# Pair 7 of the second up stage as seven half-size products, in both MLPs

## The chip, the cores and the metric

The kernel runs on one core of a Trainium2 chip. The metric is the time of the device for one execution, in microseconds (us), median of several runs. The engines named below are TensorE (PE, with its weight loads PEld), VectorE (DVE), ScalarE (ACT), GpSimd (POOL) and SyncE (SP), which issues most loads.

## The reference, cut to what matters

The program is a decoder of two layers on 512 tokens of width 1024: a gated short convolution with an MLP, then an attention block with an MLP, all in float32. What the change touches is the MLP of both layers:

```python
def squared_relu_mlp(h, w1, w2):
    return jnp.square(jax.nn.relu(h @ w1)) @ w2

x = x + squared_relu_mlp(rms_norm(x, norm_mlp[layer]), mlp_w1[layer], mlp_w2[layer])
```

`h` is 512 x 1024, `w1` is 1024 x 4096 and `w2` is 4096 x 1024. After the first MLP the residual is normalised and projected with `w_kv` for the attention; after the second comes the last norm and the output.

## The kernel before, in words

Every matrix is split into a high and a low half-precision part, and a product is three matmuls: high x high, high x low, low x high. The weights come from HBM in float32 pieces; ACT writes the high part (L219, L239) and DVE the low part (L220, L240).

The hidden width of 4096 is done in two halves. Each half is an up stage of eight column pairs (256 columns of `w1` each) and a down stage of four parts, p = 0 to 3, each with eight chunks of the hidden width. The order is: up half 0, down half 0, up half 1, down half 1 (`first_half`, and then `mlp_down` again).

A column pair is made in one of two ways. The ordinary way (`pair`) is 8 chunks x 2 x 3 matmuls of 128 x 128 weights on 512 columns, into two banks of PSUM. The other (`seven`) treats weights and activations as 2 x 2 blocks and makes 7 products of half-size blocks in place of 8 (the scheme of Strassen and Winograd): 7 x 4 chunks x 3 matmuls on 256 columns, into three banks, A, C and E. For this it needs sums of blocks of the activations (made once, in the up stage of half 0), and sums of blocks of the weights (`block_sums`, three instructions on DVE per piece, L156 and L158), so that a weight piece is converted as 7 blocks x 2 chunks x 128 = 1792 columns in place of 1024. ACT copies some products out of PSUM (L694), and DVE adds them up (L709, L712, L716). The down stage works by seven products throughout.

Behind a pair, `put_relu` makes the squared ReLU: max or min on DVE (L661 after `seven`, L664 after `pair`), a square on ACT, three token sums on DVE, and the split into `rh` (ACT, L669) and `rl` (DVE, L670), which the down stage reads.

The tuple `UP_SEVEN` says which pairs of which half go by seven: before, none of half 0 and pairs 0, 2, 4 and 6 of half 1, in both layers. An ordinary pair in half 1 takes its two banks from set c, a seven takes A and C from set a and E from set b. The down stage takes banks a, a, b, b for p = 0 and 2, and c, c, d, e for p = 1 and 3.

Weight pieces stand in a list in order of use (`mlp_pieces`). Ordinary and block pieces have buffers of their own: three loaded and four converted ones of each kind. `ahead()` converts up to three block pieces or two ordinary ones ahead of their use, and `load_more` issues a load when a loaded piece has been converted. Each engine works its queue in order; the order is laid down before the run by a scheduler that may pull a later, ready instruction into a gap, unless `tc.issue_after` puts it behind a named one. That is how conversions of later pieces come early.

Around the down stage of half 1: in the first layer `done_a` adds squares for the next norm and splits the residual for `w_kv`; the last step of that norm's sum is `thirds` (L398), which a matmul of TensorE reads (L406). In the second layer `mid_b` turns finished parts token by token with transposes on TensorE (L1523) and copies on ACT (L1519, L1534), and the final norm's gains are loaded by POOL into a buffer (`rb`) that held sums of activations.

Of the kernel before, what the change touches and what calls it, by code (L numbers as in the profile page):

```python
# [11 lines left out]
F16 = mybir.dt.float16  # L12
# [11 lines left out]
SW = 256.0  # L24
# [27 lines left out]
def body(ctx, tc, x, rel_bias, norm_mix, norm_mlp, mlp_w1, mlp_w2, a_w_in, a_conv_w, a_w_out,  # L52
         kv_norm, w_kv, cmp_pe_k, cmp_pe_v, phi_k_w1, phi_k_w2, phi_v_w1, phi_v_w2,
         b_w_qg, b_w_o, final_norm, ident_c, onehot_c, out):
    nc = tc.nc
# [4 lines left out]
    work = ctx.enter_context(pool("work"))  # L60
# [5 lines left out]
    turn = [0]  # L66

    def bank(tag, shape=(128, 512)):
        n = {"a": 2, "b": 2, "c": 2, "d": 1, "e": 1}[tag]
        return psum.tile(list(shape), F32, name=tag, bufs=n)  # L70

    def acc():
        turn[0] += 1
        return bank("aabbcc"[turn[0] % 6])
# [14 lines left out]
    def mlp_pieces(layer):  # L89

        for half in range(2):
            for p in range(8):
                (blocks if p in UP_SEVEN[half] else block)(mlp_w1[layer], (8 * half + p) * 256, SW)
            for p in range(4):
                down_blocks(mlp_w2[layer], p, half)

# [8 lines left out]
            pieces.append(([v[c + k, :, :, c0:c0 + 256] for k in range(2)], None, scale))  # L105

    BY_SEVEN = ((2, 2), (3, 0), (3, 2))
    UP_SEVEN = ((), (0, 2, 4, 6))

    v = a_w_in[0].rearrange("(c p) (s n) -> c p s n", p=128, s=3)  # L110
    for c in range(8):
# [151 lines left out]
    def ahead():  # L263
        while pos["cv"] < len(pieces) and pos["cv"] < pos["use"] + (AHEAD2[0] if blocked(pos["cv"]) else AHEAD):
            yield from convert_piece()

    def drain(gen):
        for _ in gen:
            pass
# [3 lines left out]
    wk = [first.__enter__()]  # L273
# [164 lines left out]
    xs = new_split(wk[0], "x0")  # L438
# [72 lines left out]
    for p in range(4):  # L511
        pc, pu, pb = [], [], []
        if p == 0:
# [10 lines left out]
            cv = convert_piece()  # L524
# [44 lines left out]
        for i, dst in enumerate((pc, pu, pb)):  # L569
# [19 lines left out]
            for m in range(2):  # L589
# [9 lines left out]
                elif dst is pu:  # L599
                    if m == 0:  # L600
                        convs = []
                    v = ftile("cv_v", 2, S + 2)
# [8 lines left out]
                else:  # L611
                    b = ftile("cv_b", 2)
# [12 lines left out]
    xs = new_split(work, "xs")  # L625
    ss = SumSq()
# [15 lines left out]
    def small_w():  # L642
        return (wk[0].tile([128, 2, 256], F32, name="dn_w", bufs=1), wk[0].tile([128, 256], F32, name="dn_p", bufs=1))

    def mlp_up(xs, ss, rh, half, rb, sums, gname):
        turn[0] = 1

        def root_rows():
            nonlocal rb
            rb = row_tile(broadcast_rows(ss.r), math.sqrt(SR) / (SW * SX))  # L650

        def new_z():
            return wk[0].tile([128, 8, 256], F32, name="ml_z", bufs=2)

        def put_relu(p, ph, z):
            t = z[:, 0:4].rearrange("p (m k) n -> p m (k n)", m=2)
            if len(ph) == 1:
                r = rb.rearrange("p (k n) -> p k n", k=2)
                for op, o, v, w in ((OP.max, z[:, 2:4], z[:, 2:4], r), (OP.min, z[:, 0], z[:, 0], r[:, 0]),
                                    (OP.min, z[:, 1], ph[0], r[:, 1])):  # L660
                    DVE.scalar_tensor_tensor(o, v, 0.0, w, op0=op, op1=OP.mult)  # L661
            else:
                for m in range(2):
                    DVE.scalar_tensor_tensor(t[:, m], ph[m], 0.0, rb, op0=OP.max, op1=OP.mult)  # L664
            yield
            ACT.activation(t, t, AF.Square)
            token_sums(z)
            yield
            ACT.activation(rh[0][:, p], z[:, 1:8], AF.Copy)  # L669
            DVE.tensor_tensor(rh[1][:, p], z[:, 1:8], rh[0][:, p], op=OP.subtract)  # L670

        def seven(xs, z, post):

            ws = [next_piece(), next_piece()]
            cv = ahead()
            A, C, E = bank("a"), bank("a"), bank("b")

            def product(ps, i, first):
                a, b = i
                for c in range(4):  # L680
                    wh, wl = (u[:, c % 2, a - 1] for u in ws[c // 2])
                    if b >= 4:
# [12 lines left out]

            next(post, None)
            product(A, (1, 1), True)
            kept = keep(1, A)
            with tc.issue_after(kept.ins):
                next(cv, None)  # L700
            product(C, (4, 4), True)
            keep(5, C)
            product(A, (5, 5), False)
            kept = keep(2, A)
            with tc.issue_after(kept.ins):
                next(post, None)
                next(cv, None)
            product(E, (3, 3), True)
            DVE.tensor_tensor(z[:, 3], E[:, 0:256], kept_at[1], op=OP.add)  # L709
            product(A, (6, 6), False)  # L710
            kept = keep(3, A)
            DVE.tensor_tensor(z[:, 0], kept_at[3], kept_at[5], op=OP.add)  # L712
            with tc.issue_after(kept.ins):
                drain(post)
            product(C, (7, 2), False)
            DVE.tensor_tensor(z[:, 2], C[:, 0:256], kept_at[2], op=OP.add)  # L716
            drain(cv)
            product(A, (2, 7), False)
            return [A[:, 0:256]]

        def places():

            for pool_, name, n in 4 * ((wk[0], "up_s", 4),) + ((work, "ssacc", 1), (work, "sq", 1)) + 2 * ((work, "rb", 3),):
                yield pool_.tile([128, 4, 256], F16, name=name, bufs=n)

        held, post = None, iter(())
        if half == 0:
            ss.thirds()
        for p in range(8):
            if p in UP_SEVEN[half]:  # L730
                z = new_z()
                post = put_relu(p, seven(xs, z, post), z)
                continue
            drain(post)
            ph = [bank(" c c cbc"[p]) for _ in range(2)] if half else [acc(), acc()]
            mid = {1: {1: ss.rstd, 4: root_rows}}.get(p) if half == 0 else None
            pair(xs, ph, mid=mid)
            drain(ahead())
            if p == 0 and half == 0:
                held = ph  # L740
                continue
            if held:
                drain(put_relu(0, held, new_z()))
                held = None
            post = put_relu(p, ph, new_z())
            if p + 1 not in UP_SEVEN[half]:
                drain(post)
            if half == 0 and p >= 4:
                if p == 4:
                    at = list(places())  # L750
                    sums.extend([at[2 * k], at[2 * k + 1]] for k in range(4))
                form_sums(sums, p - 4, gname, new_z(), turned_sums)
        drain(post)
        turn[0] = 5
        return rb
# [90 lines left out]
            next(post)  # L846
        drain(post)

    def first_half(hp, xs, ss, gname):
        rh = tuple(hp.tile([128, 8, 7, 256], F16, name=n) for n in ("rh", "rl"))  # L850
        sums = []
        rb = mlp_up(xs, ss, rh, 0, None, sums, gname)
        mlp_down(rh, None)
        mlp_up(xs, ss, rh, 1, rb, sums, gname)
        return rh

    xkv, xq = None, None
    with pool("hidden_a") as hp:
        wk[0] = hp
        rh = first_half(hp, xs, ss, "mlp0")  # L860
        xkv = new_split(work, "xs")
        ss = SumSq()

        def done_a(p):
            for m in range(2):
                ss.add(X[:, 2 * p + m])
            for m in range(2):
                yield
                split_gain(xkv, 2 * p + m, X[:, 2 * p + m], "kv")

        mlp_down(rh, done_a)


    with pool("attn") as ap:
# [579 lines left out]
        for i in range(len(items) + 6):  # L1454
# [39 lines left out]
    xs = xm  # L1494
    ss = ss2


    with pool("hidden_b") as hp:
        wk[0] = hp
        rh = first_half(hp, xs, ss, "mlp1")  # L1500
        xsh, xsl = (work.tile([128, 2, D], F32, name=n) for n in ("xsh", "xsl"))
        xt = [(xsh, xsl)[t // 2][:, t % 2] for t in range(4)]
        fng = [work.tile([128, S], F32, name="rb", bufs=3) for _ in range(2)]
# [162 lines left out]
```

## Time and profile before

| | |
|---|---|
| median of three runs | 1084.83 us (1084.77 to 1084.89) |
| the profiled execution | 1085.08 us |
| its span, first to last instruction | 1083.3 us |
| TensorE busy | 1070.7 us, 99% |
| DVE busy | 947.1 us, 87% |
| ACT busy | 615.6 us, 57% |
| granted TensorE clock, mean | 0.998 |

The profile is of one execution. The span is what the trace covers; the rest of the 1085.08 us lies around it. A row of the chain of waits has a start, a duration and what ran. A row of a stretch has the busy time of each engine with the number of its instructions, then the granted clock, the busy share of the DMA engines and GB/s. A row of a timeline has a start, a duration, the engine, the line, the operation, output and inputs with their shape, a count, and in brackets the idle time of the engine before it with what ended it. Durations of neighbouring instructions on one engine overlap a little, so the time from start to start is what one costs.

### The profile page before, as it was taken

The numbers are of one execution on the slowest core, as the hardware profiler recorded it, in microseconds if no ns is written. First come the engines' busy times: TensorE is split into PE (matmuls) and PEld (weight loads), VectorE is DVE, ScalarE is ACT, GpSimd is POOL, SyncE is SP. The second block draws the span as 40 slices with busy tenths as digits, with TensorE's granted clock in tenths as the row PEclk, the third lists the DMA queues.
The fourth block names the chain that finished last, engine by engine and source line by source line (L and its number), as shares of the span: only waits on it lengthen the run. The fifth ranks groups of instructions, "written<-read, shape, count | busy, mean of one in ns | idle before, by whom it ended". The sixth has DMA issues, their size and how long they took to land.

```text
span 1083.3 us, 20976 instructions
## 1 busy us (share of the span) xinstructions
PE 1070.7 (99%) x8378; PEld 729.8 (67%) x8378; DVE 947.1 (87%) x1658; ACT 615.6 (57%) x962; POOL 67.9 (6%) x109
## 2 busy tenths in 40 slices
PE   9999999999999999999999999999999999999997
PEld 4446644446887768884867677775444788766886
DVE  5898756998999999989478899996999899999886
ACT  5663243665434575448577887874656533565353
POOL 1000000000000000000110104221000000000022
PEclk9999999999999999999999999999999999999999
DMA  8344125431334335203443442201553133422221
GB/s 259 114 147 130 40 86 167 143 112 35 120 117 136 98 100 175 98 22 97 126 138 102 141 138 81 60 21 59 161 159 108 58 109 119 125 92 85 97 80 79
DMA packets 117283, 117.45 MB, mean 108 GB/s; under 512 B 7117, under 2 KB 114337, under 8 KB 117185
## 3 DMA queue, kind: packets, MB, share of 16 engines
q1 hardware_dynamic: 114288, 110.77, 32.7%
q10 hardware_dynamic: 2512, 4.70, 1.4%
q8 instruction: 66, 1.08, 0.4%
q0 software_dynamic: 384, 0.63, 0.2%
q14 instruction: 33, 0.26, 0.1%
HBM read 110.22 MB, written 2.14 MB: 104 GB/s over the span
## 4 chain that ended last, share of the span: by engine, by line
PE 90%; DVE 4%; ACT 3%; issue 1%; POOL 1%; DMA 0%; ACTq 0%; DVEq 0%; POOLq 0%
PE c L801 7%; PE a L801 7%; PE c L410 6%; PE c L411 6%; PE c L412 6%; PE a L687 6%; PE b L801 5%; PE a L412 5%; PE a L410 5%; PE a L411 5%; PE b L412 4%; PE b L410 4%; PE b L411 4%; PE d L801 4%; PE c L1308 3%; PE e L801 2%
## 5 line engine op out<-in xcount | busy, mean ns | idle before, releaser
L219 ACT ACTIVATE whi<-wst 128x1792 f16<-128x1792 f32 x86 | 145.1, 1694 | 126.1 <-DVE wst L158 51.2
L801 PEld LDWEIGHTS <-whi 128*128 128x128 f16 x1768 | 173.0, 98 | 20.3
L220 DVE SCALAR_TENSOR_TENSOR wlo<-wst,whi 128x1792 f16<-128x1792 f32 x86 | 173.3, 2019 | 12.8 <-ACT whi L219 12.8
L240 DVE SCALAR_TENSOR_TENSOR wlo<-wst,whi 128x1024 f16<-128x1024 f32 (+4 forms) x124 | 136.4, 1107 | 24.3 <-ACT whi L239 24.0
L239 ACT ACTIVATE whi<-wst 128x1024 f16<-128x1024 f32 (+4 forms) x124 | 117.3, 954 | 70.6 <-PE a L411 22.2
L412 PEld LDWEIGHTS <-wlo 128*128 128x128 f16 x848 | 82.7, 98 | 92.2 <-DVE wlo L240 1.0
L410 PEld LDWEIGHTS <-whi 128*128 128x128 f16 x848 | 82.8, 98 | 84.9 <-ACT whi L239 0.7
L411 PEld LDWEIGHTS <-whi 128*128 128x128 f16 x848 | 82.9, 98 | 84.4
L801 PEld LDWEIGHTS <-wlo 128*128 128x128 f16 x884 | 86.5, 98 | 10.9 <-issue 0.4
L412 PE MATMUL c<-xsh,wlo 128*128 128x512 f16 x224 | 84.9, 379 | 0.0
L410 PE MATMUL c<-xsh,whi 128*128 128x512 f16 x224 | 84.9, 379 | 0.0
L411 PE MATMUL c<-xsl,whi 128*128 128x512 f16 x224 | 84.9, 379 | 0.0
L669 ACT ACTIVATE rh<-ml_z 128x1792 f16<-128x1792 f32 x32 | 54.2, 1693 | 53.0 <-DVE ml_z L164 53.0
L1295 ACT ACTIVATE at_p<-at_s,at_m 128x384 f32<-128x384 f32 (+3 forms) x128 | 71.1, 557 | 21.4 <-DVE at_m L1293 20.8
L158 DVE TENSOR_TENSOR wst<-wst 128x256 f32<-128x256 f32 x172 | 72.4, 427 | 2.8
L670 DVE TENSOR_TENSOR rl<-ml_z,rh 128x1792 f16<-128x1792 f32 x32 | 64.5, 2019 | 8.0 <-ACT rh L669 7.9
L801 PE MATMUL a<-rh,wlo 128*128 128x256 f16 x256 | 69.1, 273 | 0.0
L801 PE MATMUL a<-rh,whi 128*128 128x256 f16 x256 | 69.1, 273 | 0.0
L801 PE MATMUL c<-rh,whi 128*128 128x256 f16 x252 | 68.7, 273 | 0.0
L801 PE MATMUL c<-rh,wlo 128*128 128x256 f16 x252 | 68.7, 273 | 0.0
L801 PE MATMUL c<-rl,whi 128*128 128x256 f16 x252 | 68.7, 273 | 0.0
L156 DVE TENSOR_TENSOR wst<-wst 128x512 f32<-128x512 f32 x86 | 59.1, 690 | 10.7 <-DMA wst<-mlp_w_dram 10.3
(434 smaller groups left out, 2837.8 us busy)
## 6 DMA issues: line engine op xcount, KB each, us to landing
wst<-mlp_w_dram SPq DMA_DIRECT2D x160, 256.0 KB, 3.0
wst<-mlp_w_dram SPq DMA_DIRECT2D x48, 512.0 KB, 4.0
wst<-a_w_in_dram SPq DMA_DIRECT2D x12, 512.0 KB, 3.8
wst<-w_kv_dram SPq DMA_DIRECT2D x12, 512.0 KB, 3.8
wst<-a_w_out_dram SPq DMA_DIRECT2D x8, 512.0 KB, 3.4
wst<-b_w_qg_dram SPq DMA_DIRECT2D x8, 512.0 KB, 3.7
wst<-b_w_o_dram SPq DMA_DIRECT2D x8, 512.0 KB, 3.5
T<-ext_d ACTq DMA_DIRECT2D x6, 528.0 KB, 3.6
```

The source lines that it names most:

```text
L158: DVE.tensor_tensor(b[:, :, o], b[:, :, x], b[:, :, y], op=OP.add)
L219: ACT.activation(hi, b[:, :, 1:], AF.Copy, scale=sc)
L220: lows[0] = DVE.scalar_tensor_tensor(lo, b[:, :, 1:], sc, hi, op0=OP.mult, op1=OP.subtract)
L239: ACT.activation(hi[:, s:e], w, AF.Copy, scale=sc)
L240: DVE.scalar_tensor_tensor(lo[:, s:e], w, sc, hi[:, s:e], op0=OP.mult, op1=OP.subtract)
L410: PE.matmul(ps, w[0], xs[0], start=start, stop=False, **k)
L411: PE.matmul(ps, w[0], xs[1], start=False, stop=False, **k)
L412: return PE.matmul(ps, w[1], xs[0], start=False, stop=stop, **k)
L670: DVE.tensor_tensor(rh[1][:, p], z[:, 1:8], rh[0][:, p], op=OP.subtract)
L687: PE.matmul(ps[:, 0:256], l, r, start=first and c == 0 and n == 0, stop=c == 3 and n == 2, skip_group_check=not first)
L801: mm = PE.matmul(acc7[i], wl if n == 1 else wh, xl if n == 2 else xh, stop=c == closes[i] and n == 2, start=c == 0 and n == 0 and not othe ...
L1295: self.weighed = ACT.activation(self.p[:, w], lg[:, w], AF.Exp, bias=mn[:, j:j + 1], scale=-1.0, accum_out=l[:, br * 4 + h:br * 4 + h + 1])
```

## The change

`UP_SEVEN` gets an index for the layer, and pair 7 of half 1 joins the pairs that go by seven, in both layers; half 0 stays without. Pairs of half 1 now take turns between bank sets a and c, whichever way they are made: even pairs a, odd pairs c. So pair 7 by seven has A and C from set c, next to pair 6 with set a. The rest of the diff serves pairs by seven in half 0, which this kernel doesn't have: `early` is false and `behind` is pairs 4 to 7 as before. The buffers for sums are taken one pair at a time instead of all at once.

```diff
-                (blocks if p in UP_SEVEN[half] else block)(mlp_w1[layer], (8 * half + p) * 256, SW)
+                (blocks if p in UP_SEVEN[layer][half] else block)(mlp_w1[layer], (8 * half + p) * 256, SW)
-    UP_SEVEN = ((), (0, 2, 4, 6))
+    UP_SEVEN = (((), (0, 2, 4, 6, 7)), ((), (0, 2, 4, 6, 7)))
-        def seven(xs, z, post):
+        def seven(xs, z, post, tag):
-            A, C, E = bank("a"), bank("a"), bank("b")
+            A, C, E = bank(tag), bank(tag), bank("b")
...
-            drain(cv)
+            with nullcontext() if half else tc.issue_after(kept.ins):
+                drain(cv)
...
+        by_seven = UP_SEVEN[layer][half]
+        early = half == 0 and layer == 0 and by_seven
+        behind = range(1, 5) if by_seven else range(4, 8)
...
         for p in range(8):
-            if p in UP_SEVEN[half]:
+            own = half or by_seven and p >= by_seven[0]
+            tag = ("c" if tag == "a" else "a") if own else "bca"[p % 3]
+            if p in by_seven:
                 z = new_z()
-                post = put_relu(p, seven(xs, z, post), z)
+                post = put_relu(p, seven(xs, z, post, tag), z)
                 continue
             drain(post)
-            ph = [bank(" c c cbc"[p]) for _ in range(2)] if half else [acc(), acc()]
+            ph = [bank(tag) for _ in range(2)]
...
-            if p + 1 not in UP_SEVEN[half]:
+            if p + 1 not in by_seven:
                 drain(post)
-            if half == 0 and p >= 4:
-                if p == 4:
-                    at = list(places())
-                    sums.extend([at[2 * k], at[2 * k + 1]] for k in range(4))
-                form_sums(sums, p - 4, gname, new_z(), turned_sums)
+            if half == 0 and not early and p in behind:
+                sums.append(next(at))
+                form_sums(sums, p - behind[0], gname, new_z(), turned_sums)
```

## Rows read from the trace of the kernel before

**Rows 1.** The page: busy us, share of the span, instructions of each engine.
```profile
PE 1070.7 (99%) x8378; PEld 729.8 (67%) x8378; DVE 947.1 (87%) x1658; ACT 615.6 (57%) x962; POOL 67.9 (6%) x109
```

**Rows 2.** The chain of waits, behind the first MLP and in the second.
```profile
489.95 0.28 PE d L406 x12
...
977.89 3.93 PE a L687 x36
...
987.06 0.22 PE c L410
...
997.42 1.31 PE a L801 x12
...
1054.56 0.28 ACT xsl L1534
```

**Rows 3.** Stretches of the first MLP: pairs 6 and 7, four down parts.
```profile
389.29:408.82 19.53, 19.53 (x135) 12.91 (x133) 18.14 (x25) 13.77 (x16) 0.00 (x0) 1.00 0.30 99
408.82:427.16 18.34, 18.34 (x171) 16.44 (x169) 17.89 (x23) 10.75 (x9) 0.00 (x0) 1.00 0.51 158
427.16:445.50 18.34, 18.34 (x171) 16.43 (x169) 17.83 (x27) 7.47 (x7) 0.00 (x0) 1.00 0.39 130
445.50:463.84 18.34, 18.34 (x171) 16.45 (x169) 17.18 (x30) 9.21 (x9) 0.00 (x0) 1.00 0.34 115
463.84:482.18 18.34, 18.34 (x170) 16.39 (x168) 15.83 (x27) 6.31 (x8) 0.00 (x0) 1.00 0.01 2
```

**Rows 4.** Stretches of the second MLP: pair 6, pair 7, three down parts.
```profile
977.89:987.06 9.17, 9.17 (x85) 8.16 (x84) 9.13 (x15) 4.99 (x8) 0.00 (x0) 1.00 0.02 6
987.06:997.42 10.36, 10.36 (x50) 4.75 (x49) 10.12 (x12) 7.04 (x6) 2.27 (x3) 1.00 0.45 143
997.42:1015.76 18.34, 18.34 (x170) 16.44 (x169) 14.73 (x16) 8.05 (x7) 0.00 (x0) 1.00 0.20 63
1015.76:1034.10 18.34, 18.34 (x170) 16.52 (x169) 14.36 (x25) 7.51 (x16) 3.25 (x4) 1.00 0.26 88
1034.10:1054.80 20.70, 20.70 (x190) 18.53 (x189) 19.40 (x26) 11.07 (x20) 1.80 (x1) 1.00 0.31 103
```

**Rows 5.** The timeline of DVE, second MLP: what its steps cost.
```profile
979.78 1.28 DVE L664 SCALAR_TENSOR_TENSOR ml_z<-c,rb 128x512 f32<-128x512 f32 x2
...
986.58 0.41 DVE L716 TENSOR_TENSOR ml_z<-a,dn_w 128x256 f32<-128x256 f32 x1
986.92 1.01 DVE L661 SCALAR_TENSOR_TENSOR ml_z<-ml_z,rb 128x256 f32<-128x256 f32 x2
...
988.19 2.01 DVE L670 TENSOR_TENSOR rl<-ml_z,rh 128x1792 f16<-128x1792 f32 x1
...
1016.45 0.68 DVE L156 TENSOR_TENSOR wst<-wst 128x512 f32<-128x512 f32 x1
...
1017.97 0.42 DVE L767 SCALAR_TENSOR_TENSOR dn_w<-a,dn_p 128x256 f32<-128x256 f32 x1
```

**Rows 6.** The timeline of DVE, first MLP and the norm behind it.
```profile
408.56 1.22 DVE L240 SCALAR_TENSOR_TENSOR wlo<-wst,whi 128x1024 f16<-128x1024 f32 x1
...
423.74 1.28 DVE L240 SCALAR_TENSOR_TENSOR wlo<-wst,whi 128x512 f16<-128x512 f32 x2
...
473.90 2.02 DVE L220 SCALAR_TENSOR_TENSOR wlo<-wst,whi 128x1792 f16<-128x1792 f32 x1
475.84 0.42 DVE L780 TENSOR_TENSOR X<-X,dn_w 128x256 f32<-128x256 f32 x1
...
488.74 0.69 DVE L398 TENSOR_TENSOR rb<-sq 128x512 f32<-128x512 f32 x1
```

**Rows 7.** Whom DVE waited for, 977 to 1050: total us, times, longest.
```profile
DVE wst L156 <- DMA wst<-mlp_w_dram: 3.3, 2, 1.8
DVE wlo L220 <- ACT whi L219: 2.2, 1, 2.2
```

More of the change, by code (lines that the diff above doesn't have):

```diff
@@ L643, in small_w, with mlp_up @@
         return (wk[0].tile([128, 2, 256], F32, name="dn_w", bufs=1), wk[0].tile([128, 256], F32, name="dn_p", bufs=1))
-    def mlp_up(xs, ss, rh, half, rb, sums, gname):
-        turn[0] = 1
+    def mlp_up(xs, ss, rh, layer, half, rb, sums):
+        gname = f"mlp{layer}"
         def root_rows():
@@ L721, in places, with early_sums, move_sums @@
         def places():
-            for pool_, name, n in 4 * ((wk[0], "up_s", 4),) + ((work, "ssacc", 1), (work, "sq", 1)) + 2 * ((work, "rb", 3),):
-                yield pool_.tile([128, 4, 256], F16, name=name, bufs=n)
-        held, post = None, iter(())
+            tags = 4 * ((wk[0], "up_s", 4),) + ((work, "ssacc", 1), (work, "sq", 1)) + 2 * ((work, "rb", 3),)
+            for i in range(0, 8, 2):
+                yield [u.tile([128, 4, 256], F16, name=name, bufs=n) for u, name, n in tags[i:i + 2]]
+        def early_sums(c):
+            if c < 2:
+                sums.append(next(at))
+                form_sums(sums, c, gname, new_z(), turned_sums)
+            else:
+                staged_sums[c] = [u[:, 4 + c, 0:4] for u in rh]
+                form_sums(staged_sums, c, gname, new_z(), turned_sums)
+        def move_sums():
+            for c in (2, 3):
+                sums.append(next(at))
+                for u, v in zip(sums[c], staged_sums[c]):
+                    nc.gpsimd.dma_start(u, v)
+        at, staged_sums = places(), {}
+        by_seven = UP_SEVEN[layer][half]
+        early = half == 0 and layer == 0 and by_seven
+        behind = range(1, 5) if by_seven else range(4, 8)
+        held, post, tag = None, iter(()), ""
         if half == 0:
@@ L738, in mlp_up @@
             drain(ahead())
+            if early and p < 2:
+                for c in (2 * p, 2 * p + 1):
+                    early_sums(c)
             if p == 0 and half == 0:
@@ L745, in mlp_up @@
             post = put_relu(p, ph, new_z())
-            if p + 1 not in UP_SEVEN[half]:
+            if p + 1 not in by_seven:
                 drain(post)
-            if half == 0 and p >= 4:
-                if p == 4:
-                    at = list(places())
-                    sums.extend([at[2 * k], at[2 * k + 1]] for k in range(4))
-                form_sums(sums, p - 4, gname, new_z(), turned_sums)
+            if early and p == 2:
+                move_sums()
+            if half == 0 and not early and p in behind:
+                sums.append(next(at))
+                form_sums(sums, p - behind[0], gname, new_z(), turned_sums)
         drain(post)
@@ L847, in mlp_down, with first_half @@
         drain(post)
-    def first_half(hp, xs, ss, gname):
+    def first_half(hp, xs, ss, layer):
         rh = tuple(hp.tile([128, 8, 7, 256], F16, name=n) for n in ("rh", "rl"))
         sums = []
-        rb = mlp_up(xs, ss, rh, 0, None, sums, gname)
+        rb = mlp_up(xs, ss, rh, layer, 0, None, sums)
         mlp_down(rh, None)
-        mlp_up(xs, ss, rh, 1, rb, sums, gname)
+        mlp_up(xs, ss, rh, layer, 1, rb, sums)
         return rh
@@ L859, in body @@
         wk[0] = hp
-        rh = first_half(hp, xs, ss, "mlp0")
+        rh = first_half(hp, xs, ss, 0)
         xkv = new_split(work, "xs")
@@ L1499, in body @@
         wk[0] = hp
-        rh = first_half(hp, xs, ss, "mlp1")
+        rh = first_half(hp, xs, ss, 1)
         xsh, xsl = (work.tile([128, 2, D], F32, name=n) for n in ("xsh", "xsl"))
```

## The prediction

> **What bounds the kernel now.** I read the page first. TensorE is busy in 99% of the span and VectorE (DVE) in 87% [rows 1]. A busy TensorE says little by itself, so I went to the chain of waits around the second up stage of the second MLP. There every link is a matmul: the stretch of seven products of pair 6 starts at 977.89 us, pair 7 (full size) at 987.06, the down stage at 997.42 [rows 2]. So pair 6 costs 9.17 us and pair 7 10.36 us, and nothing stands between them. Third, the stretches: in all ten that I cut out of the two MLPs TensorE is busy for the whole stretch and the granted clock is 1.00 [rows 3, 4]. TensorE therefore sets the end, and a microsecond of its work that goes is a microsecond of the kernel, as long as the others keep up. The reader is to see in the same rows who is closest to not keeping up: DVE, with 9.13 of 9.17 us and 10.12 of 10.36 us in the up stage, and 17.89, 17.83 and 17.18 of 18.34 us in the first three quarters of the first MLP's down stage. ScalarE (ACT) has 7.04 of 10.36 us, and the DMA engines are at 0.51 of their time at the most.
>
> **The change, part by part.** (1) In both layers column pair 7 of the second up stage goes from 8 chunks x 2 x 3 = 48 matmuls of 512 columns to 7 products x 4 x 3 = 84 of 256 columns. The first took 10.36 us (216 ns each), the second takes what pair 6 takes, 9.17 us (109 ns each) [rows 2]: 1.19 us less per layer, 2.38 us for both. That is all that the change can give directly.
>
> One rule speaks against this. The Trainium skill, "TensorE: Matmul & The Clock Gate", section "Back-to-back issue gap", says that in a stream of weight loads and matmuls the sustained spacing is about 81 ns at 128 columns and 131 ns at 512. By that 48 long matmuls would take 6.3 us, and 84 at 256 columns, an estimate on the line between the two figures of the Trainium skill (98 ns), 8.2 us: the change would lose 1.9 us per layer. The rows show 216 and 109 ns, so the measurement decides and the rule falls here.
>
> (2) DVE gets more to do, for pair 7 of each layer. Its two weight pieces are now turned into seven block forms. Such a piece costs DVE three block sums, 1.52 us from the first sum at 1016.45 to the next instruction at 1017.97 [rows 5], and a low part of 1792 columns, 1.94 us from 473.90 to 475.84 [rows 6]: 3.46 us. An ordinary piece costs one low part of 1024 columns, 1.22 us as recorded at 408.56, or 1.14 without the overlap of 0.08 that the longer one shows (2.02 recorded). Two pieces: 6.92 - 2.28 = +4.64 us. The outputs: three adds that put the products together, 0.34 us each (986.58 to 986.92), and the three max/min steps of 1.27 us (986.92 to 988.19) in place of the two of 1.28 us at 979.78 [rows 5]: +1.01 us. Squares, token sums and the split into rh and rl stay. Together +5.65 us of DVE per layer, in which TensorE now spends 1.19 us less. DVE is thus asked for 6.84 us of its idle time per layer. This is the price of the edit, and the question is who pays it.
>
> (3) First MLP. Over pairs 6 and 7 and the down stage DVE is idle for 1.39 + 0.45 + 0.51 + 1.16 + 2.51 = 6.02 us [rows 3]. 6.84 are wanted: 0.8 us are missing. What is late next? The last down piece's low part starts at 473.90 and ends at 475.84; TensorE comes to it two chunks before the stage's end, at 482.18 - 2 x 2.29 = 477.6 [rows 3, 6]. So the lead is down to 1.8 us there already. Behind the down stage the norm's sum of squares follows, whose last step on DVE starts at 488.74 and takes 0.69 us, and TensorE's matmul on it starts at 489.95 [rows 2, 6]: 0.5 us of cover. In between DVE converts four later w_kv pieces (first at 408.56, last at 423.74, some 4.7 us) that TensorE needs only after 482 [rows 6]; they can move back, but not past the sum of squares altogether. The bounds of the stall in this layer: 0 if the idle time closes up and the w_kv work moves; 6.84 - 1.76 = 5.1 us if none of it does. I take the 0.8 us that the balance lacks, since the row of the whole stretch is the nearest.
>
> (4) Second MLP. Here DVE is idle for 0.04 + 0.24 + 3.61 + 3.98 + 1.30 = 9.17 us from pair 6 to 1054.80 [rows 4], 2.3 us more than is wanted. There are two soft spots. Two of the idle times, 3.3 us together, are waits for a weight load [rows 7]; a load starts only when DVE has finished with the buffer, so it may slip along with DVE and the wait come back. Without these 3.3 us the balance is 1.0 us short. And the chain passes from ACT's copy at 1054.56 straight to TensorE [rows 2]: there is no cover at that point, and whatever DVE and ACT still owe arrives at the end. DVE's one wait of 2.2 us for a high part [rows 7], however, is set by ACT's copies of transposes that TensorE makes, so there the chain starts afresh if DVE has caught up by then. Bounds: 0 and 6.8 us; I take 0.3 us, near the lower end, as the balance is positive.
>
> (5) Moved steps. The low and high parts of the first two down pieces now stand behind those of pair 7: the four buffers for converted block pieces hold pairs 6 and 7 when pair 6 runs, so at the start of the down stage two down pieces are converted and not four. The third is needed 2 x 4.59 = 9.2 us into the stage and DVE needs 3.46 us for each of two, so I cost this at nothing beyond (3) and (4); if DVE is 5.7 us late at that point, one piece is just in time. The loads of pair 7 become four DMAs of 256 KB for two of 512 KB: the same bytes, on DMA engines that are at 0.45 in that stretch [rows 4]. The final norm's gains (POOL's two loads) and ACT's scaled identity wait for the last reader of the sums' buffers, now the end of pair 7 instead of pair 6, 9.17 us later; they are first used when the down stage's first quarter is done, 18 us on, so nothing. ACT gets two longer conversions and four copies of a product. That is less than DVE's 5.65 us, since each of these has a dearer partner there, and ACT is idle for 3.32 us in pair 7's stretch and 10.29 us in the next [rows 4]: nothing. Pair 7 also adds an order on ACT: pair 6's squares stand behind the copy of pair 7's third product, and its rh behind that of the fifth, 3.9 and 6.6 us into the pair, with conversions of down pieces queued behind them. The down stage reads this rh at its seventh chunk, 13.8 us into it: nothing again.
>
> (6) The banks. Pair 7 takes its two accumulators from set c while pair 6's sit in set a, so its first product need not wait for pair 6's last DVE step. Their third bank is of set b for both; the down stage takes both b banks, and it reaches the one of pair 7 with its seventh product, 18 matmuls or 1.96 us into the stage. The product in it is complete 5.24 us into pair 7, so there are 9.17 + 1.96 - 5.24 = 5.9 us. DVE must have read it by then: cover enough unless DVE is late by nearly all of its extra work. Pairs 1, 3 and 5 stay in c. I cost it at nothing; gone, it would be 1 us or so.
>
> **The sum.** -2.38 + 0.8 + 0.3 = -1.3 us. The profiled execution took 1085.08 us (span 1083.3 and 1.8 around it), which gives 1083.8; the median of the three runs is 0.25 us lower, so 1083.5 us.
>
> **The rivals.** (A) *DVE hides everything*: both layers keep 1.19 us, 1082.4 us. For it: the 4.7 us of w_kv conversions that can move, and 9.17 us idle in the second MLP. Against: 6.02 < 6.84 in the first. (B) *A wait takes the place of the work*: DVE's idle time closes only by half, 3.0 us in the first layer and 4.6 in the second. The stalls are 3.8 - 1.8 = 2.0 us and 2.2 us, net +1.8: 1086.6 us; with a little more closed it comes out at 1085. For it: all listed idle times are waits for ACT or a load, so they are made by the order of the queues and not by lack of work. (C) *DVE becomes the bound*, the slower side: in the first MLP's down stage DVE's queue never catches up, as the lead of the last converted piece is down to 1.8 us before the change. The place is the last quarter of the down stage, the price 5.1 us there at most, and from 3.4 us of total stall less 2.38 the kernel is slower by 1 us, from 4.6 us by more than 0.2%. With 5.1 us in the first and 2.2 in the second: 1089.7 us. For it: 97% busy stretches. Against: the movable w_kv work. (D) *Half-size products run into their weight loads.* If a load of 97 ns no longer hid beside its matmul of 109 ns, 84 of both would take 17.3 us, 6.9 us more than the pair: up to 1098.7 us, and anything between. For it: the loads fill 8.16 of pair 6's 9.17 us. Against: TensorE is full all that time at 109 ns a product [rows 4], in a stretch of the very kind that is added, so this is all but excluded. By the estimate from the Trainium skill's section above it would be 1.9 us per layer and 1088.6 us.
>
> **How the numbers follow.** My forecast (partly eaten, gain 0.3 to 2.1 us) 0.42; A 0.27; B 0.17; C 0.13; D 0.01. A measurement of this kernel can tell about 0.2%, 2.17 us, from no change. Faster by that is A alone: 0.27. Slower by that is C, D and 0.02 of B, whose own figure lies just below it: 0.16. The rest, 0.57, is within. The range: low is A and 0.2 us for what else may shift, 1082.2; the high end takes in B up to just below its own figure, 1086.4, and leaves out most of C. The forecast's own range is 1082.7 to 1084.5.
>
> **What would show it.** Right: the chain shows pair 7 in 9.2 us with 84 products of set c and b; DVE above 98% busy from pair 6 to the end of the first down stage, short gaps of TensorE (together under 1 us) in its last quarter or at the sum of squares, and the w_kv conversions later than 425. A would show as no gap at all in either MLP. B and C show as gaps of TensorE released by a low part on DVE; if pair 7's first product waits, (6) is wrong. The prediction is wrong if TensorE's gaps in the two MLPs add up to over 3 us, or if the time changes by more than the gaps and 2.38 us explain, that is, in the attention between.

## The result, and the profile after

The changed kernel is slower: median 1092.26 us (1091.28 to 1094.15, six runs) against 1084.84 (1084.42 to 1085.17, six runs) for the kernel before on the same chip. The ratio is 1.0069, 95% interval 1.0058 to 1.0079. The forecast was 1083.5, with a range up to 1086.4. The profiled execution of the changed kernel took 1093.24 us, its span is 1091.5, 8.2 over the one before. Line numbers of the profile move by 28 in the lower part of the file: the down stage is now L829 (was L801), its sums L795 (L767), the transposes L1551 (L1523), the token copies L1547 and L1562 (L1519, L1534).

Where the 8.2 us arise, from the starts of the stages (before: [rows 2 to 4]; after: the stretches below):

| stretch | before | after | difference |
|---|---|---|---|
| start to pair 6, first MLP | 389.29 | 389.50 | +0.2 |
| pairs 6 and 7, first MLP | 19.53 | 21.40 | +1.9 |
| down stage, first MLP | 73.36 | 75.44 | +2.1 |
| norm and attention, to pair 6, second MLP | 495.71 | 496.16 | +0.45 |
| pairs 6 and 7, second MLP | 19.53 | 18.40 | -1.1 |
| the rest | 85.88 | 90.60 | +4.7 |

The page, engines (as [rows 1]): 1.9 us more on TensorE, though it has less to do, and 10 more on DVE.

```profile
PE 1072.6 (98%) x8450; PEld 737.4 (68%) x8450; DVE 957.3 (88%) x1678; ACT 620.6 (57%) x970; POOL 69.9 (6%) x109
```

Stretches after the change, in the columns of [rows 3] and [rows 4]: pairs 6 and 7 and four equal parts of the down stage of the first MLP; pairs 6 and 7 and three parts of the second, then the stretch in which its fourth down part begins.

```profile
389.50:410.90 21.40, 18.59 (x169) 16.36 (x168) 21.30 (x31) 13.71 (x17) 0.00 (x0) 1.00 0.51 161
410.90:429.76 18.86, 18.47 (x170) 16.29 (x169) 17.77 (x26) 9.39 (x7) 0.00 (x0) 1.00 0.21 69
429.76:448.62 18.86, 18.86 (x176) 16.88 (x174) 18.50 (x30) 9.64 (x10) 0.00 (x0) 1.00 0.43 138
448.62:467.48 18.86, 17.82 (x164) 15.72 (x162) 17.02 (x27) 8.28 (x9) 0.00 (x0) 1.00 0.27 88
467.48:486.34 18.86, 18.80 (x173) 16.57 (x172) 17.32 (x29) 8.23 (x10) 0.00 (x0) 1.00 0.09 29
...
982.50:1000.90 18.40, 18.40 (x170) 16.45 (x169) 16.42 (x23) 11.19 (x14) 0.00 (x0) 1.00 0.18 59
1000.90:1019.20 18.30, 18.30 (x170) 16.39 (x168) 17.82 (x26) 9.81 (x8) 3.22 (x3) 1.00 0.36 116
1019.20:1037.60 18.40, 18.39 (x168) 16.25 (x167) 17.84 (x26) 9.33 (x17) 2.85 (x3) 1.00 0.37 125
1037.60:1058.30 20.70, 20.70 (x188) 18.23 (x187) 19.47 (x31) 8.95 (x7) 1.68 (x2) 1.00 0.36 117
1058.30:1068.00 9.70, 6.89 (x49) 5.26 (x47) 9.63 (x13) 5.69 (x15) 4.96 (x4) 0.82 0.02 6
```

The reader is to see three things. In the first row DVE is busy for 21.30 of 21.40 us and TensorE is not. In the row at 982.50 pair 7 by seven gives what it should, 18.40 for 19.53, with no gap. In the last row the second MLP loses everything at one point, and the granted clock there is 0.82.

For whom TensorE waited (total us, times, longest): first the first MLP from 375 to 490, then the second. Before the change neither stretch had such a row.

```profile
PE a L687 <- ACT dn_p L694: 2.4, 1, 2.4
PE a L829 <- DVE wlo L220: 1.4, 2, 1.0
PE c L687 <- ACT dn_p L694: 0.4, 1, 0.4
...
PE c L829 <- ACT xsh L1562: 2.4, 1, 2.4
PE c L829 <- ACT xsl L1562: 0.5, 1, 0.5
```

From start to start of TensorE's matmuls the gaps are 5.1 us in the first MLP (2.5 in pair 6, 0.6 in pair 7, 2.0 in the down stage) and 3.1 in the second; there about 1.5 us more come from matmuls at the lower clock behind the gap. That is 9.7, less 2.4 for the fewer matmuls; 0.2 at the start and 0.45 in the norm and the attention make 8.0 of the 8.2.

The largest wait of the first MLP is a copy of ACT that stands in the queue behind something else. The timeline of ACT in pair 6:

```profile
385.10 1.14 ACT L239 ACTIVATE whi<-wst 128x512 f16<-128x512 f32 x2
390.29 1.70 ACT L669 ACTIVATE rh<-ml_z 128x1792 f16<-128x1792 f32 x1 [4.05 <-DVE ml_z L164]
393.14 1.15 ACT L239 ACTIVATE whi<-wst 128x512 f16<-128x512 f32 x2 [1.15 <-DMA wst<-w_kv_dram]
394.19 0.36 ACT L694 ACTIVATE dn_p<-a 128x256 f32<-128x256 f32 x1
```

TensorE's third product, which goes into the bank that is copied, waits for the copy at 394.19 (L694). Ahead of it stands a conversion of `w_kv` (393.14), which waits for its load, and ahead of that the `rh` of pair 5, which waited 4.05 us for DVE. DVE was late with that because it, too, had `w_kv` in its queue, here between the token sums of pair 5:

```profile
387.18 1.22 DVE L240 SCALAR_TENSOR_TENSOR wlo<-wst,whi 128x1024 f16<-128x1024 f32 x1
388.31 0.42 DVE L164 TENSOR_TENSOR ml_z<-ml_z 128x256 f32<-128x256 f32 x1
388.65 1.22 DVE L240 SCALAR_TENSOR_TENSOR wlo<-wst,whi 128x1024 f16<-128x1024 f32 x1
389.78 0.41 DVE L164 TENSOR_TENSOR ml_z<-ml_z 128x256 f32<-128x256 f32 x1
```

Before, these conversions were at 408.56 to 423.74 [rows 6]. Pair 7's pieces no longer pass through the ordinary buffers, so the `w_kv` pieces behind them in the list get the buffers a pair earlier, and the scheduler, which fills gaps with what is ready, puts them there.

The 1.4 us in the down stage are of the same kind, in DVE's queue. From 389 to 490 DVE waits 2.9 us for weight loads, 0.5 before the change, and both low parts for which TensorE waits stand behind block sums that had waited so. The longer one:

```profile
451.38 0.69 DVE L156 TENSOR_TENSOR wst<-wst 128x512 f32<-128x512 f32 x1 [1.80 <-DMA wst<-mlp_w_dram]
451.99 2.02 DVE L220 SCALAR_TENSOR_TENSOR wlo<-wst,whi 128x1792 f16<-128x1792 f32 x1
```

ACT had written the high part of this piece by 449.72. The load that the block sums wait for went out at 445.95, when DVE had given its buffer free: what is late on DVE comes back to it as a later load.

In the second MLP it is again ACT's queue, at the end of the third down part:

```profile
1056.18 3.28 ACT L219 ACTIVATE whi<-wst 128x1792 f16<-128x1792 f32 x2 [2.86 <-DVE wst L158]
1059.37 0.36 ACT L1547 ACTIVATE ml_z<-c 128x256 f32<-128x256 f32 x1
...
1061.59 0.43 ACT L1562 ACTIVATE xsl<-c 128x256 f32<-128x256 f32 x1
```

Two conversions wait for DVE's block sums; behind them stand the token copies that free the bank of the fourth down part. Their transposes were over at 1053.9, 5.5 us before. The same two conversions before the change, in ACT's timeline:

```profile
1049.00 3.28 ACT L219 ACTIVATE whi<-wst 128x1792 f16<-128x1792 f32 x2 [2.86 <-DVE wst L158]
```

They are 7.2 us later now, while TensorE is 4.3 us later there (its products go on behind the transposes at 1053.69, before at 1049.44): DVE is 2.9 us further behind, and all of it arrives at the first matmul into that bank.

### The profile page after: what moved, and what is told of

It is laid out like the page before. It is cut to its first block, busy times and chain, and to the rows that moved or that the text cites. A ratio compares the mean times of both kernels' runs of the same rounds, so it can differ in the third digit from the quotient of the medians.

```text
span 1091.5 us, 21172 instructions
## 1 busy us (share of the span) xinstructions
PE 1072.6 (98%) x8450; PEld 737.4 (68%) x8450; DVE 957.3 (88%) x1678; ACT 620.6 (57%) x970; POOL 69.9 (6%) x109
## 3 DMA queue, kind: packets, MB, share of 16 engines
q8 instruction: 66, 1.08, 0.4%
## 4 chain that ended last, share of the span: by engine, by line
PE 72%; DVE 19%; ACT 3%; issue 3%; DMA 2%; POOL 0%; SPq 0%; ACTq 0%; DVEq 0%; POOLq 0%
DVE wlo L220 6%; PE c L410 5%; PE c L411 5%; PE c L412 5%; PE a L410 5%; PE a L412 5%; PE a L411 4%; PE c L829 4%; PE a L829 4%; PE b L410 4%; PE b L411 4%; PE b L412 4%; PE b L829 3%; PE c L1336 3%; PE a L687 2%
## 5 line engine op out<-in xcount | busy, mean ns | idle before, releaser
L219 ACT ACTIVATE whi<-wst 128x1792 f16<-128x1792 f32 x90 | 151.7, 1692 | 147.6 <-DVE wst L158 64.8
L220 DVE SCALAR_TENSOR_TENSOR wlo<-wst,whi 128x1792 f16<-128x1792 f32 x90 | 181.4, 2021 | 11.6 <-ACT whi L219 11.5
L829 PEld LDWEIGHTS <-whi 128*128 128x128 f16 x1768 | 173.3, 98 | 20.9
L239 ACT ACTIVATE whi<-wst 128x1024 f16<-128x1024 f32 (+4 forms) x120 | 113.1, 951 | 70.4 <-PE a L411 22.2
L240 DVE SCALAR_TENSOR_TENSOR wlo<-wst,whi 128x1024 f16<-128x1024 f32 (+4 forms) x120 | 131.4, 1102 | 24.4 <-ACT whi L239 24.2
L410 PEld LDWEIGHTS <-whi 128*128 128x128 f16 x816 | 79.8, 98 | 81.1 <-issue 0.6
L411 PEld LDWEIGHTS <-whi 128*128 128x128 f16 x816 | 79.7, 98 | 81.1
L829 PEld LDWEIGHTS <-wlo 128*128 128x128 f16 x884 | 86.6, 98 | 16.4 <-DVE wlo L220 5.1
L158 DVE TENSOR_TENSOR wst<-wst 128x256 f32<-128x256 f32 x180 | 76.8, 434 | 2.3
L411 PE MATMUL c<-xsl,whi 128*128 128x512 f16 x192 | 72.8, 379 | 0.0
L412 PE MATMUL c<-xsh,wlo 128*128 128x512 f16 x192 | 72.8, 379 | 0.0
L410 PE MATMUL c<-xsh,whi 128*128 128x512 f16 x192 | 72.8, 379 | 0.0
L829 PE MATMUL c<-rh,whi 128*128 128x256 f16 x252 | 68.9, 274 | 2.8 <-ACT xsh L1562 2.4
L156 DVE TENSOR_TENSOR wst<-wst 128x512 f32<-128x512 f32 x90 | 62.4, 697 | 10.1 <-DMA wst<-mlp_w_dram 9.8
L829 PE MATMUL a<-rh,wlo 128*128 128x256 f16 x256 | 69.2, 273 | 1.4 <-DVE wlo L220 1.4
L829 PE MATMUL a<-rh,whi 128*128 128x256 f16 x256 | 69.1, 273 | 0.0
L829 PE MATMUL c<-rh,wlo 128*128 128x256 f16 x252 | 69.0, 274 | 0.1
L829 PE MATMUL c<-rl,whi 128*128 128x256 f16 x252 | 69.0, 274 | 0.0
```

What stands on the lines that cost most here:

```text
L156: DVE.tensor_tensor(b[:, :, 4:7:2], b[:, :, 0:1].to_broadcast(two), b[:, :, 2:0:-1], op=OP.add)
L158: DVE.tensor_tensor(b[:, :, o], b[:, :, x], b[:, :, y], op=OP.add)
L219: ACT.activation(hi, b[:, :, 1:], AF.Copy, scale=sc)
L220: lows[0] = DVE.scalar_tensor_tensor(lo, b[:, :, 1:], sc, hi, op0=OP.mult, op1=OP.subtract)
L239: ACT.activation(hi[:, s:e], w, AF.Copy, scale=sc)
L240: DVE.scalar_tensor_tensor(lo[:, s:e], w, sc, hi[:, s:e], op0=OP.mult, op1=OP.subtract)
```

## The experiments

Two causes stand against each other. Q: the order of the queues, that is, conversions that wait ahead of copies that TensorE needs. V: DVE's amount of work, wherever it is put. A third, that the rest of the diff costs something, falls with the traces of the first two runs: outside the layer that has the new pair every engine runs the same operations on the same tiles in the same order as in the kernel before (l1_only up to 970 us, l0_only behind its first MLP), and the first MLP of l1_only takes 92.9 us from pair 6 to the end of its down stage, as before. All times are medians of 5 to 11 executions beside the kernel before, which lay at 1084.98 to 1085.08.

**Each layer alone.**

```diff
-    UP_SEVEN = (((), (0, 2, 4, 6, 7)), ((), (0, 2, 4, 6, 7)))
+    UP_SEVEN = (((), (0, 2, 4, 6, 7)), ((), (0, 2, 4, 6)))     # l0_only
+    UP_SEVEN = (((), (0, 2, 4, 6)), ((), (0, 2, 4, 6, 7)))     # l1_only
```

> Pair 7 by seven in the first MLP alone; the second MLP as before. Theory Q (the order of ACT's queue: conversions that wait for a load or for DVE stand ahead of a copy that TensorE needs) and theory V (VectorE lacks 5.65 us per layer, wherever it is put) both give here what the changed kernel lost up to the attention, 4.8 us less 0.4 us of start: 1084.8 + 4.4 = 1089.2 us, with gaps of TensorE of about 5 us in pairs 6, 7 and the down stage and none in the second MLP. If the two layers act on each other, it lies over 1 us off this.

> Pair 7 by seven in the second MLP alone. Both theories: the second layer's share of the loss, 8.2 - 4.8 = 3.4 us, 1088.2 us, with one group of gaps of about 3 us behind the second down part and the lower granted clock after it, and none in the first MLP. With l0_only it should add up to the changed kernel: 4.4 + 3.4 = 7.8 us over before.

1088.47 us (ratio 1.0033, 1.0022 to 1.0044) and 1086.68 (1.0014, 1.0005 to 1.0023): +3.4 and +1.6, each under what was expected, and together 5.0 of the 7.4. In l1_only the gaps are 2.6 us, and the lower clock doesn't come behind them. The trace of l0_only shows the other reason. It has the gap of 2.6 us in pair 6, but no gap of the down stage; in its place TensorE runs at the lower clock behind the gap. The same stretch, first of the changed kernel, then of l0_only:

```profile
395.00:398.00 3.00, 3.00 (x30) 2.68 (x29) 3.00 (x5) 2.63 (x4) 0.00 (x0) 1.00 0.19 68
```
```profile
395.00:398.00 3.00, 3.00 (x16) 2.06 (x15) 3.00 (x5) 2.05 (x4) 0.00 (x0) 0.50 0.23 81
```

One execution gets through 30 matmuls in 3 us, the other through 16. The 1.7 us lost there look like time for DVE to catch up: in copies_first, too, the lower clock follows this gap and the first MLP has no later one. No run separates the two. So an execution pays part of its loss at one place or at another, and the loss by stages differs between executions.

**w_kv held back.** ACT's conversions of the first four `w_kv` pieces behind its copy of pair 7's fifth product:

```diff
             kept = keep(3, A)
+            kept7[0] = kept.ins
...
-                ACT.activation(hi[:, s:e], w, AF.Copy, scale=sc)
+                with tc.issue_after(kept7[0]) if kv_at <= i < kv_at + 4 else nullcontext():
+                    ACT.activation(hi[:, s:e], w, AF.Copy, scale=sc)
```

> The changed kernel, with ACT's conversions of the first four w_kv pieces tied behind its copy of pair 7's fifth product, so that they can't stand in pairs 5 and 6; nothing else is changed. Theory Q: the gaps of 2.5 and 0.6 us in pairs 6 and 7 go, and the shorter ones in the down stage (2.0 us together) stay or grow by up to 1 us, since the same DVE work now lies there: 1089.2 to 1090.2 us. Theory V: the same work on DVE, so the stall only moves into the down stage: 1092.3 us, within 0.6.

1090.14 us (1.0044, 1.0032 to 1.0057): 2.1 below the changed kernel, as Q said, at the upper end. Stretches from pair 6 to the norm, and TensorE's waits:

```profile
389.20:407.50 18.30, 18.30 (x169) 16.41 (x168) 17.63 (x25) 12.21 (x15) 0.00 (x0) 1.00 0.21 69
...
426.25:445.00 18.75, 18.75 (x174) 16.80 (x173) 18.75 (x30) 10.08 (x12) 0.00 (x0) 1.00 0.44 143
445.00:463.80 18.80, 18.69 (x172) 16.52 (x170) 18.80 (x30) 9.20 (x9) 0.00 (x0) 1.00 0.45 143
463.80:482.60 18.80, 17.98 (x164) 15.64 (x162) 18.70 (x32) 8.01 (x9) 0.00 (x0) 1.00 0.17 52
```
```profile
PE c L829 <- DVE wlo L220: 0.8, 1, 0.8
PE d L406 <- DVE rb L398: 0.5, 1, 0.5
```

Pairs 6 and 7 now take 18.30 us without a gap: the order was what cost 3.1 us there. But in the last three of these stretches DVE is busy for 56.25 of 56.35 us, and TensorE waits for it. From the start of pair 6 to the end of the norm behind the down stage the layer takes 108.8 us, for 112.0 in the changed kernel and 107.7 before: the order took 3.2 us. What is left, 1.1 us more than before and the 1.19 us of the gain, goes with waits for a DVE that is hardly idle.

**Token copies first.** In the second MLP, the conversions behind the token copies in the third down part too:

```diff
-                        behind = squared if p == 1 else None
+                        behind = squared if p < 3 else None
```

> The changed kernel, with ACT's conversions that follow in the second MLP's third down part tied behind the token copies of that part (as they are already in the second part); nothing else is changed. Theory Q: TensorE's gap of 3.1 us at the fourth down part goes and with it the 1.5 us at the lower clock, less up to 1 us for conversions that now come later: 1087.7 to 1088.7 us. Theory V: DVE is what is late, and the gap comes back some microseconds later at a low part: 1091.5 to 1092.5 us.

1089.67 us (1.0045, 1.0033 to 1.0058), between the two. The gap at the fourth down part is gone, and 10 us later a smaller one comes up, where the transposes wait for DVE's sums of part 2:

```profile
PE a L1551 <- DVE X L808: 1.7, 1, 1.7
PE a L1551 <- DVE X L810: 0.3, 1, 0.3
PE c L829 <- DVE dn_w L1585: 0.3, 1, 0.3
```

**Both, then with less work for DVE.** both_held has the two edits. held_pool adds GpSimd for pair 7's block sums; held_nolow leaves out pair 7's low parts; after_nolow does that in the changed kernel's own order.

```diff
-                block_sums(b)
+                block_sums(b, POOL if i in fifth else DVE)                  # held_pool
...
-            lows[0] = DVE.scalar_tensor_tensor(lo, b[:, :, 1:], sc, hi, op0=OP.mult, op1=OP.subtract)
-            ready[i] = (hi, lo)
+            if i not in fifth: lows[0] = DVE.scalar_tensor_tensor(lo, ...)  # held_nolow, after_nolow
+            ready[i] = (hi, lo or hi)
```

> The two edits of kv_held and copies_first together; all work is done. From their traces: with w_kv held the first layer still takes 1.1 us more than before from pair 6 to the attention (108.8 against 107.7), with the copies first the second takes 1.3 us more to the end (106.9 against 105.6). If the two don't act on each other: 1085.0 + 2.4 = 1087.4 us, 0.5 either way. If a purely ordering cause remained (theory Q as first stated), it would be 1082.5.

> As both_held, with the block sums of pair 7's two pieces of each layer on GpSimd in place of VectorE: DVE is relieved of 3.0 of the 5.65 us per layer, all work is done. If what is left after the ordering is DVE's amount of work (theory V): the stalls of about 2.3 and 2.5 us per layer shrink by what DVE is relieved of, 1082.6 to 1084.0 us, a gain over before. If GpSimd's sums come late (a sum of 128x256 on it takes 0.7 to 2.3 us) or slow DVE beside them: 1087 to 1090 us, with TensorE waiting for pair 7's weights.

> As both_held, but the low parts of pair 7's weights are not made in either layer: TensorE reads the high part in their place, the same number of matmuls. DVE is relieved of 2 x 1.94 = 3.9 of the 5.65 us per layer and of nothing else. Theory V: the stalls left go and both layers show the 1.19 us of the fewer matmuls: 1082.4 to 1083.2 us. If it is not DVE's amount of work, it stays at both_held, 1087.4 us.

> The changed kernel in its own order, with the low parts of pair 7's weights left out as in held_nolow. Theory V (only the amount counts): as held_nolow, 1082.4 to 1083.2 us. Theory Q: the w_kv conversions still wait for their load ahead of the product copy, and pair 6 keeps its gap of 2.5 us (with the lower clock after it 4.2), while the stalls in the down stages go: 1085.3 to 1087.0 us.

1089.86 us (1.0044, 1.003 to 1.0058), 1088.86 (1.004, 1.0027 to 1.0052), 1085.55 (1.0006, 0.9997 to 1.0014) and 1091.07 (1.0057, 1.0045 to 1.007).

both_held misses its 1087.4: it is no better than either edit alone. Its trace has the 1.7 and 0.3 us of copies_first, and then the lower clock. The stretch behind that wait, first in copies_first, then in both_held:

```profile
1068.00:1072.00 4.00, 4.00 (x38) 3.61 (x39) 1.00 (x3) 2.93 (x13) 2.65 (x4) 1.00 0.00 0
```
```profile
1068.00:1072.00 4.00, 4.00 (x23) 2.95 (x22) 0.91 (x1) 2.80 (x13) 2.77 (x4) 0.57 0.01 2
```

held_pool has the same waits of TensorE as both_held, within 0.1 us, and one of 0.3 us more. So its 1.0 us is not shown to come from GpSimd: the lower clock is in the trace of both_held and not in this one.

held_nolow takes 3.9 us per layer from DVE and gains 4.3 us in all over both_held: amount counts. Two things go with it that no run separates: pair 7's low parts need no buffers either, and the lower clock of both_held is missing. after_nolow takes away the same work and gains 1.2, and 5.5 us lie between it and held_nolow: order counts as much. In its trace one row holds nearly the whole loss of the first MLP; it is again the copy of a first product, now pair 7's, and ahead of it in ACT's queue stands pair 6's `rh`, which waited 5.13 us for DVE's token sums:

```profile
PE c L687 <- ACT dn_p L694: 3.9, 1, 3.9
```
```profile
400.65 0.69 DVE L156 TENSOR_TENSOR wst<-wst 128x512 f32<-128x512 f32 x1 [4.10 <-DMA wst<-mlp_w_dram]
401.26 0.42 DVE L164 TENSOR_TENSOR ml_z<-ml_z 128x256 f32<-128x256 f32 x1
...
401.77 1.70 ACT L669 ACTIVATE rh<-ml_z 128x1792 f16<-128x1792 f32 x1 [5.13 <-DVE ml_z L164]
```

I had expected that gap in pair 6; it moved to the next pair. And here DVE is not busy: it stands idle for 4.10 us at block sums that wait for their load, with the last token sum behind them. That load went out at 395.67, behind one of `w_kv` at 395.25 in SP's queue, which had waited for DVE to finish a `w_kv` piece; in held_nolow it went out at 393.11, and the block sums found it there. So the order counts in three queues, ACT's, DVE's and that of the loads.

Neither Q nor V alone gives these four times. Both count: DVE is late, by its work or by a wait in its own queue, and an order in which ACT's queue passes its lateness on to copies needed at once makes several microseconds of it. Even held_nolow, with 1.8 us per layer more on DVE than before, shows nothing of the 2.4 us. In its second MLP TensorE waits 0.8, 0.3 and 0.3 us at the places of copies_first; what that edit costs without the added work on DVE was not run.

**Another place.** The fifth seven in half 0 in place of half 1, as pair 5 (with `own = half` and `early = False`, so that half 0 keeps its bank sets), in one layer or both:

```diff
+    UP_SEVEN = (((), (0, 2, 4, 6)), ((5,), (0, 2, 4, 6)))      # half0_l1; half0_l0, half0_both alike
```

> Pair 7 of half 1 back to the ordinary way in both layers; in place of it pair 5 of the first up stage (half 0) of the second MLP by seven, in the bank sets that this stage has anyway; the activations' sums are made behind pairs 1 to 4. It asks DVE for the same 6.8 us, but from pair 5 to the end of that half's down stage DVE is idle for some 8.1 us, ACT has no w_kv conversions there and no token copies follow. If the fifth product stage fails only because of where it was put: 1.2 us faster than before, 1083.8 us (half that if some idle time doesn't close). If DVE's idle time can't be used at all, as in the second MLP's end: 1 to 3 us slower, 1086 to 1088 us.

> The same in the first MLP alone (pair 5 of half 0 by seven, pair 7 of half 1 ordinary in both layers). DVE is idle for about 8.5 us from there to the end of that down stage. Placement theory: 1083.8 us; no usable idle time: 1086 to 1088 us.

> Both together. Placement theory: 2.4 us faster than before, 1082.6 us, which would beat both kernels; otherwise the sum of the two losses, 1087 to 1091 us.

1086.68 us (1.0014), 1089.08 (1.0038) and 1091.34 (1.0058): slower, so as put, the placement theory missed. But in the trace of half0_l1 all waits of the second MLP lie inside the new seven (819 to 826); there is none over 0.2 us behind it, in the stages in which DVE had to make up its 6.8 us. What TensorE waits for is product copies, here in half0_l1, and in half0_l0 also the activations' sums, made just before (3.8 us in four waits; the second fence shows the longest):

```profile
PE a L687 <- ACT dn_p L694: 2.0, 1, 2.0
PE a L687 <- ACT up_k L694: 0.4, 1, 0.4
```
```profile
PE a L687 <- ACT ssacc L431: 1.7, 1, 1.7
```

So one pair later, when the sums are done (pair 5 takes banks b and pair 6 banks a):

```diff
+    UP_SEVEN = (((), (0, 2, 4, 6)), ((6,), (0, 2, 4, 6)))      # pair6_l1; pair6_l0, pair6_both alike
+            tag = ... else ("bcabcbac" if by_seven else "bcabcabc")[p]
```

> As half0_l1, but the fifth seven of the second MLP is pair 6 of half 0 (bank set a, with pair 5 in set b and pair 7 in c), 10 us behind the last of the activations' sums. Place theory: no gap in pair 6, DVE's backlog closes in the down stage as in half0_l1: 1085.0 - 1.2 = 1083.8 us. Amount theory: gaps of 2 us or more in the down stage, 1086 to 1088 us.

> The same in the first MLP alone. Place theory: 1083.8 us. Amount theory: 1086 to 1088 us.

> Both MLPs. Place theory: 1082.6 us, faster than before and than the changed kernel. Amount theory: 1087 us or more.

1084.46 us (0.9996, 0.9987 to 1.0005), 1084.83 (1.0, 0.9991 to 1.0009) and 1085.27 (1.0003, 0.9994 to 1.0012): no loss any more, but no gain that can be told. 6 us of pair6_both against half0_both come from one pair's distance to the sums, with the bank order that goes with it. Its MLPs still wait at two kinds of places:

```profile
PE a L687 <- ACT dn_w L694: 1.2, 2, 0.7
PE c L829 <- ACT xsl L1562: 0.5, 1, 0.5
PE c L829 <- ACT xsh L1562: 0.3, 1, 0.3
```

The first is a buffer: at the first seven of half 1, ACT's copy into `dn_w` waits until DVE has read there the sums of the last down part. pair6_z keeps two products in free rows of `ml_z` instead; pair6_zcf adds the edit of copies_first.

```diff
-            two, one = small_w()
+            two, one = z[:, 4:6], wk[0].tile([128, 256], F32, name="dn_p", bufs=1)
```

> As pair6_both, but a seven keeps its second and fifth product in two free rows of its own ml_z instead of the buffer dn_w. Place theory: the gaps of 0.9 and 0.7 us at the first seven of half 1 go, 1085.2 - 1.6 = 1083.6 us, faster than before by over 1 us. If the backlog of DVE stands behind them, the wait only moves on by a few products: 1085.2 us.

> pair6_z with the edit of copies_first as well. Place theory: the 0.9 us at the fourth down part go too, 1082.7 us. If DVE has no time there either, its sums of part 2 come late for the transposes as in copies_first (1.7 and 0.3 us): 1084 to 1086 us.

1083.77 us (0.9988, 0.9979 to 0.9997) and 1084.59 (0.9997, 0.9989 to 1.0006). pair6_z came out as expected: 1.25 us under the kernel before and 8.5 under the changed kernel. It beats both, though by little: 1.25 of the 2.38 us, and the interval of its ratio ends at 0.9997. Holding conversions behind the token copies took 0.8 us of that back, again by transposes that wait for DVE (0.6 and 0.3 us).

## Why the prediction was wrong, point by point

(1) *The 1.19 us per layer* were right: pairs 6 and 7 take 18.40 us in the second MLP (1.13 less) and 18.30 in kv_held. 168 matmuls of 256 columns in 18.30 us are 109 ns each; by the prediction's estimate from the spacing in the Trainium skill, "TensorE: Matmul & The Clock Gate", section "Back-to-back issue gap", the change would have lost 1.9 us here; the trace does not agree.

(2) *DVE's 5.65 us* were about right, if a little high: on the page it is busy for 10.2 us more, 5.1 per layer, and from pair 6 to the end of the first down stage for 91.9 us in place of 86.9 [rows 3].

(3) *First MLP, 0.8 us missing* is the step that failed most. TensorE's work in the stretch is 19.53 - 1.19 + 73.36 = 91.7 us and DVE's is 91.9. That is no slack at all, and I charged only the deficit, as if idle time were free to be filled. And that the `w_kv` conversions "can move back" was wrong in direction: nothing made it move back, and the freed ordinary buffers let it move forward, into pair 6 and ahead of a product copy. The stall was 5.1 us. That equals the upper bound that I had named, but 3.1 of it lie in the up stage, where I had looked for none; kv_held shows that this part is order. Of the 2.0 us in the down stage 1.4 stand behind block sums that wait for a load.

(4) *Second MLP, 0.3 us* failed in size, at the place named as the soft spot: ACT's token copies straight to TensorE, without cover. "Near the lower end, as the balance is positive" was the wrong reason. The balance is over 77 us, the bank is needed at one instant, and what counted was how late DVE was at that instant: 2.9 us. The wait made 3.1 us of it and the lower clock 1.5 more, a term that the prediction did not have.

(5) *Moved steps at nothing*: the gains and the identity cost nothing that the trace shows. The loads did, 2.9 us of waits on DVE in the first MLP; that a load may slip along with DVE I had named for the second alone. ACT's order did, too. I had listed what is queued behind pair 7's copies and priced ACT by its idle time (3.32 us); the price is set by who waits at the head of its queue.

(6) *Banks at nothing* was right: no gap is released by a bank that DVE holds.

*The rivals.* C had the right side and named DVE's queue, at 1089.7 us; the time was 2.6 more. Its place, the last quarter of the down stage, was wrong: that quarter lost 0.2 us. B's rule, that idle time closes only in part, fits held_nolow, where 1.8 us per layer more work for DVE goes with the loss of the whole 2.4 us; for the second MLP the edit of copies_first may have a share in that. A and D are out. Of the signs named, gaps released by a low part on DVE (B and C) were 1.4 of the 8.2 us, the rest was copies of ACT; DVE above 98% held in the first MLP's pairs (21.30 of 21.40) and one part of its down stage, "`w_kv` later than 425" was the opposite, and the sign for "wrong", gaps over 3 us, came with 8.2.

What stays open: how much of the loss falls to order and how much to amount can't be split to a microsecond, since the lower clock comes in some executions and not in others, and the runs that relieved DVE of low parts freed their buffers as well.

## What to carry to other kernels

When the second-busiest engine is at 94% (here 86.9 of 92.9 us) beside a full one, its remaining idle time is not a budget: price an edit at the instants at which the first engine has no cover, by how late the second will be there, and count what stands ahead of the needed instruction in each in-order queue, that of the loads included. Freeing a buffer is an edit of the schedule as well: ask what will be pulled forward into it, and what that waits for. If a step doesn't pay where it is, the same step at a place whose inputs are long done may: here 6 us lay in one pair's distance.

## What the runs showed of the hardware

**A gap may cost a second time.** Behind nearly the same gap of TensorE (2.53 us in the changed kernel, 2.62 in l0_only, 2.33 in copies_first) the granted clock from 395 to 398 was 1.00 (2.4 GHz) in the first, 0.50 (1.2 GHz) in the second and 0.66, a mean over both levels, in the third; at the lower one the matmuls started 0.21 us apart in place of 0.11, and that took 1.7 us more. In l0_only the rows above show it.

**GpSimd slowed DVE.** In held_pool GpSimd took over 3.0 us of DVE's sums per layer, and DVE's busy time from 330.9 to 498 stayed at 161.3 us, as in both_held. DVE beside a sum of GpSimd, and without one (held_pool):

```profile
353.98 2.29 DVE L240 SCALAR_TENSOR_TENSOR wlo<-wst,whi 128x1024 f16<-128x1024 f32 x1
356.19 1.21 DVE L162 TENSOR_TENSOR ml_z<-ml_z 128x512 f32<-128x512 f32 x1
...
358.19 1.21 DVE L240 SCALAR_TENSOR_TENSOR wlo<-wst,whi 128x1024 f16<-128x1024 f32 x1
```
```profile
353.76 1.43 POOL L156 TENSOR_TENSOR wst<-wst 128x512 f32<-128x512 f32 x1 [346.03 <-DVE wst L158]
355.26 2.73 POOL L158 TENSOR_TENSOR wst<-wst 128x256 f32<-128x256 f32 x2
```

The same low part takes 2.29 us beside GpSimd and 1.21 alone. The Trainium skill, "SBUF — State Buffer", section "Who interferes with whom", says that a DVE instruction with two SBUF inputs contends with a GpSimd instruction that reads SBUF; the trace agrees, with 1.08 us on this one instruction. DVE was relieved of nothing that its busy time shows.
